# A two-layer decoder trunk on one core: seven products instead of eight for one more column group of the MLP's second eighth, with its fast steps at other places

## The chip, the cores and the metric

The kernel runs on one core of a Trainium2 chip. The metric is the device time of one execution in microseconds (us); of several runs the median is taken. The kernel before takes 2023.53 us, the median of three runs between 2023.32 and 2023.73.

## The reference, cut to what matters

256 tokens of width 2048 pass through two layers. Each has a mixing half (attention heads and gated groups) and an MLP half, and the change touches the MLP alone, D_FF being 8192:

```python
for l in range(DEPTH):
    ...
    h2 = rms_norm(x, norm2_g[l])
    x = x + jnp.square(jax.nn.relu(h2 @ w_up[l])) @ w_down[l]
return rms_norm(x, final_g)
```

Everything is float32, and a product of two float32 matrices is made on TensorE as three products of fp32r parts (high by high, low by high, high by low), so each weight and each activation is split into a high part (`hi`, an ACT copy) and a low part (`lo`, a DVE subtraction).

## The kernel before, in words

**Steps.** The whole program is one list of steps. An ordinary step multiplies one weight tile of 128 x 1024 numbers (512 KB): `Sub.load` issues its DMA on SP (L159), `Sub.high` writes `hi` on ScalarE (ACT, L168), `Sub.low` writes `lo` on VectorE (DVE, L178), and `mm` in `transposed` issues 24 matmuls on TensorE (PE, L410). Column groups of 256 fill one PSUM bank; when the last step of such a group is done, a function (`after`) empties the bank. Weights are prepared a few tiles ahead: there are seven buffers for raw tiles and six each for `hi` and `lo`, and each engine runs its instructions in the order in which the steps' loop wrote them.

**Eighths.** An MLP is worked in eight slices of 1024 hidden units. In round `e` of the loop at the end of `layer`, 16 ordinary steps make the hidden units of eighth `e` from `w_up` (four column groups of four steps, called up steps here), and eighth `e-1` is multiplied with its 1024 rows of `w_down`. For each 256 columns of hidden units, ACT applies relu (L787) and square (L790), and `to_half` makes high (ACT, L646) and low (DVE, L649).

**Fast steps.** A group of 512 output columns of `w_down` can be done by `fast` with seven half-size products instead of eight (a Winograd form of Strassen's scheme over a 2 x 2 split). It is two fast steps of 42 matmuls each (PE, L440) instead of four ordinary steps of 24. Each fast step takes four tiles: two that are loaded (`Top` and `Bottom`), and two made from them by four DVE subtractions (L219, L220, L223, L224), called upper and lower here after the names in `fast`. On the other side it needs sums of the hidden units, made by `sums` (DVE, L803 to L806) and split into high and low in `sum_parts`. The seven products lie in three and a half PSUM banks: the first column group has them in the auxiliary banks, where six add up over the rounds and only the seventh is copied out (L876); each other one uses whichever of the banks acc0 and acc1 the ordinary steps aren't filling at that moment, then acc2 and acc3 (`slots_other`), and half an auxiliary bank for the seventh product.

**What happens to the products.** For the second and third column groups, ACT copies the three banks to the SBUF tile `stage` right behind the second fast step (L908) and the seventh half bank five tiles later (L894). GpSimd (POOL) then adds them to DRAM tiles, `far` (`put`, L873), and in a group's final round adds them back and `combine` forms the outputs. `stage` is one buffer for all groups.

**Places.** `ORDER` and `USUAL` say which column groups are done by fast steps in round `e` and at which places: a pair (7, 9) puts the group's two fast steps ahead of ordinary steps 7 and 9 of that round, counted from 0. Round 1 has two groups before, at places 7 and 10 and at 13 and 14; rounds 2 to 5 follow `USUAL`, with three groups at (7, 9), (2, 3) and (13, 14). Places 0 to 15 are up steps, four to a bank, and the banks alternate between acc0 and acc1; so step 12 begins a new bank, and the bank of steps 8 to 11 is then the one that isn't being filled.

Of the kernel before, what the change touches and what calls it, by code (L numbers as in the profile page):

```python
# [29 lines left out]
F32R = mybir.dt.float32r  # L30
I32 = mybir.dt.int32
AF = mybir.ActivationFunctionType
OP = mybir.AluOpType
AX = mybir.AxisListType

P = 128
# [3 lines left out]
KC = D // P  # L40
NH = 8
# [18 lines left out]

ORDER = {1: ((7, 10), (13, 14)), 6: ((12, 15), (2, 3), (7, 8)), 7: ((7, 10), (2, 3)), 8: ()}
FINAL = (7, 7, 6)
LAST = (4, 6, 8, 10, 0, 2, 12, 14)
USUAL = ((7, 9), (2, 3), (13, 14))
# [25 lines left out]
def trunk(ctx: ExitStack, tc: tile.TileContext, layout, xT, consts, gains, w, b_sp, w_sp, out):  # L92
    nc = tc.nc
# [18 lines left out]
    shared = [None]  # L112
    ar = tp.tile([P, sum(a[1] * a[2] for a in ARENA.values()) - FIRST], F32, name="ar")
    inner_flat = ar[:, 0:2048]
    inner = inner_flat.rearrange("p (k t) -> p k t", k=NH)
# [3 lines left out]
    def new_shared(dtype):  # L119

        shared[0] = tp.tile([P, FIRST], dtype, name="shared", tag="shared", bufs=1)
# [106 lines left out]
    cols = cp.tile([P, (2 * DEPTH + 1) * KC + 2 * DEPTH * NH], F32, name="cols")  # L228
# [14 lines left out]
    def later(delay, cost, fn):  # L243

        queue.append((now[0] + delay, cost, fn))
# [118 lines left out]
    summed, sum_parts = [True], [None]  # L364
# [4 lines left out]
    def collect(fn, *args, **kw):  # L369
        n = len(steps)  # L370
        fn(*args, **kw)
        part = steps[n:]
        del steps[n:]
        return part
# [100 lines left out]
    def mark(fn):  # L475

        steps.append((None, fn, None))
# [4 lines left out]
    def from_tiles(tiles, n):  # L482
        return lambda k: tiles[k // n][0][:, k % n, :, :]

    def new_half(cell):
        cell[0] = tp.tile([P, NH, 2, S], F32R, name="half", tag="half", bufs=2)
# [15 lines left out]
    def pair(ps):  # L502
        return ps.rearrange("p (a b) -> p a b", a=2)
# [14 lines left out]
    def layer(l, n1, n2, n3, last):  # L518
# [125 lines left out]
        def to_half(t, c, src, wait=False):  # L644

            act.activation(t[:, c:c + 2, 0, :], src, AF.Copy)  # L646

            def low():
                vec.tensor_tensor(t[:, c:c + 2, 1, :], src, t[:, c:c + 2, 0, :].bitcast(F32), op=OP.subtract)  # L649

            if wait:
                behind.append((now[0] + 1, low))
            else:
                low()
# [98 lines left out]
        def wide(t):  # L753
            return t[:, None, :].to_broadcast([P, 2, S])
# [8 lines left out]
        def after_down(e, c, ps):  # L763

            if e == 8:
                update(n3, c, ps, True, last)
            elif c < 12:
                vec.tensor_tensor(pair(ps), pair(ps), wide(n2.R2), op=OP.mult)
                update(n3, c, ps, False, last)
            elif e == 1:  # L770
                act.activation(rest_sums[:, c - 12:c - 10, :], pair(ps), AF.Copy)
            else:
                y = rest_sums[:, c - 12:c - 10, :]
                vec.tensor_tensor(y, y, pair(ps), op=OP.add)
# [6 lines left out]
        def after_up(e):  # L781
            def f(c, ps):
                if hid[e][0] is None:
                    new_half(hid[e])
                z = inner[:, c // P:c // P + 2, :]
                if e < 7:
                    act.activation(z, pair(ps), AF.Relu)  # L787
                else:
                    vec.scalar_tensor_tensor(z, pair(ps), 0.0, wide(n2.R), op0=OP.max, op1=OP.mult)
                act.activation(z, z, AF.Square)  # L790
                to_half(hid[e][0], c // P, z, True)
                if c == 768:
                    summed[0] = False
                    if e == 0:
                        new_shared(F32R)
                        sum_parts[0] = shared[0].rearrange("p (k h t) -> p k h t", k=NH, h=2)
                    later(1, 1.5, sums)
            return f

        def sums():  # L800

            a11, a12, a21, a22 = (inner[:, 4 * k:4 * k + 4, t * P:(t + 1) * P] for t in range(2) for k in range(2))
            vec.tensor_tensor(a22, a21, a22, op=OP.add)  # L803
            vec.tensor_tensor(a21, a11, a21, op=OP.subtract)
            vec.tensor_tensor(a11, a22, a11, op=OP.subtract)
            vec.tensor_tensor(a12, a12, a11, op=OP.subtract)  # L806

            def parts(k):
                to_half(sum_parts[0], k, inner[:, k:k + 2, :])
                summed[0] = k == 6  # L810

            for k in range(0, 8, 2):
                later(0, 0.6, lambda k=k: parts(k))

        def combine(place, c, banks, o=None):

# [46 lines left out]
        def slots_other(g, banks):  # L863
            seventh = sevenths()[g - 1]
            banks[:] = [acc_bank(1 - bank_at[0]), acc_bank(2), acc_bank(3)]
            return [h for b in banks for h in halves(b)] + [seventh]

        far = [dp.tile([P, 256 if g == 0 else 7 * 256], F32, name=f"far{l}{g}") for g in range(3)]

        def put(e, g, r):  # L870

            src = stage[:, r] if g else stage_one
            nc.gpsimd.dma_start(far[g][:, r], src, **({} if e == max(g, 1) else {"accum_op": OP.add}))  # L873

        def seventh_out(e, o):
            act.activation(stage_one, o[6], AF.Copy)  # L876
            put(e, 0, slice(0, 256))

        def first_done(e):
            def f(o):  # L880
                if e < 7:
                    soon(5, lambda: seventh_out(e, o))
                else:
                    soon(10, lambda: nc.gpsimd.dma_start(stage[:, 1536:1792], far[0]))
                    soon(15, lambda: combine(stage, 0, [aux_bank] * 2, o))
                    for i, c in enumerate((12, 14)):
                        soon(17 + 2 * i, lambda c=c: rest_in(c))
            return f

        def other_done(e, g, banks):  # L890
            here = [lambda i=i: acc_bank(i) for i in (2, 3)]

            def rest(o):
                act.activation(stage[:, 1536:1792], o[6], AF.Copy)  # L894
                for i in range(4):
                    soon(2 * i, lambda r=slice(512 * i, min(512 * (i + 1), 1792)): move(r))
                if e == FINAL[g]:
                    soon(9, lambda: combine(stage, 4 * g, here))

            def move(r):  # L900
                if e < FINAL[g]:
                    put(e, g, r)
                else:
                    nc.gpsimd.dma_start(stage[:, r], far[g][:, r], accum_op=OP.add)

            def f(o):
                for i in range(3):
                    act.activation(stage[:, 512 * i:512 * (i + 1)], banks[i], AF.Copy)  # L908
                soon(5, lambda: rest(o))
            return f  # L910

        base = len(steps)
        for e in range(9):
            up, down, quick = [], [], []
            if e == 8:
                mark(lambda: bank_at.__setitem__(0, 1))
            if e < 8:
                up = collect(transposed, "w_up", l, 0, KC, e * 1024, 1024, from_hs, after_up(e), of=2)
            if e:
                w = 512 * len(ORDER.get(e, USUAL))  # L920
                hidden = [hid[e - 1]]
                down = collect(transposed, "w_down", l, (e - 1) * 1024, 8, w, D - w, from_tiles(hidden, NH),
                               lambda c, ps, e=e, w=w: after_down(e, (c + w) // P, ps),
                               apart=last and e == 8, of=2 if e < 8 else 4,
                               cols=None if e < 8 else [c * P for c in LAST])
                for g, at in enumerate(ORDER.get(e, USUAL)):
                    banks = []
                    quick += zip(at, collect(fast, "w_down", l, (e - 1) * 1024, 512 * g, hidden,
                                             (lambda g=g, banks=banks: slots_other(g, banks)) if g else slots_first,
                                             (0, 2, 4, 6) if g or e == 1 else (6,), range(7) if g or e == 7 else (6,),  # L930
                                             other_done(e, g, banks) if g else first_done(e)))
            quick = dict(quick)
            for i, one in enumerate(up + down):
                if i in quick:
                    steps.append(quick[i])
                steps.append(one)
# [13 lines left out]
    for l in range(DEPTH):  # L950
        layer(l, norms[2 * l], norms[2 * l + 1], norms[2 * l + 2], l == DEPTH - 1)
# [80 lines left out]
    n = norms[-1]  # L1032
# [3 lines left out]
    for c, w in [(0, 1), (1, 1)] + [(c, 2) for c in range(2, KC, 2)]:  # L1036
        r = slice(c, c + w)
# [38 lines left out]
```

## Time and profile before

| | |
|---|---|
| median of the runs | 2023.53 us (2023.32 to 2023.73) |
| the profiled execution's own time | 2023.7 us |
| its span, first to last instruction | 2021.9 us |
| mean granted TensorE clock | 0.997 |
| busy: PE, DVE, ACT, POOL | 99%, 78%, 60%, 8% of the span |

The profile is one execution. Between the span and that execution's own time lie 1.8 us. Times in the rows are microseconds from the span's start; a row of a timeline or of the chain gives start, length, engine, line, operation, and a bracket for idle time ahead of it and what ended it. Matmuls overlap each other, so PE shows as busy while it is fed without a gap; how fast it runs is read from many matmuls in a row. The numbering of the lines is that of the kernel before; from L792 on the changed kernel's numbers are 2 to 4 higher.

### The profile page before, as it was taken

What the parts mean: (1) busy time and instruction counts of PE and PEld (TensorE: products, weight loads), DVE (VectorE), ACT (ScalarE), POOL (GpSimd) and SP (SyncE); (2) the same over time, 40 slices, a digit from 0 to 9 for tenths busy, and PEclk for the clock granted to TensorE, in tenths of its full rate; (3) what the DMA queues carried; (4) which work ended last, traced back from release to release, by engine and by line L of the source; (5) the groups of instructions that cost most, each with busy time, mean ns of one, the idle gap of its engine ahead of it and who ended that gap; (6) DMA issues with size and microseconds to landing.
All of it is one profiled execution on the core that took longest, in us unless ns stands there. A gap on an engine that the chain in (4) does not pass through costs nothing.

```text
span 2021.9 us, 40716 instructions
## 1 busy us (share of the span) xinstructions
PE 2009.5 (99%) x16810; PEld 1973.4 (98%) x16810; DVE 1579.8 (78%) x1954; ACT 1221.2 (60%) x1613; POOL 156.2 (8%) x200
## 2 busy tenths in 40 slices
PE   9999999999999999999999999999999999999997
PEld 8998999999999999999989989999999999999997
DVE  7566766688888898898856667667888898888985
ACT  7565455566566666665645654556666666667653
POOL 0002300000001000100000032000000000010000
PEclk9999999999999999999999999999999999999998
DMA  9555556566678776866664555565676776777662
GB/s 330 192 167 167 187 189 202 174 229 204 222 219 239 240 225 203 249 215 215 201 215 158 168 187 188 188 199 179 217 229 208 228 236 216 239 220 241 212 215 81
DMA packets 126442, 419.26 MB, mean 207 GB/s; under 512 B 14128, under 2 KB 22064, under 8 KB 126256
## 3 DMA queue, kind: packets, MB, share of 16 engines
q1 hardware_dynamic: 110800, 389.86, 57.2%
q0 software_dynamic: 14304, 23.86, 6.5%
q8 instruction: 131, 2.15, 0.4%
q10 hardware_dynamic: 1152, 2.94, 0.4%
q14 instruction: 55, 0.45, 0.1%
HBM read 394.58 MB, written 22.02 MB: 206 GB/s over the span
## 4 chain that ended last, share of the span: by engine, by line
PE 99%; DVE 0%; ACT 0%; issue 0%; DVEq 0%
PE acc L410 70%; PE acc L440 10%; PE aux L440 8%; PE acc L470 3%; PE acc L472 3%; PE acc L471 3%; PE aux L699 0%; PE aux L635 0%; PE aux L593 0%; PE aux L622 0%; PE aux L994 0%; DVE x L1038 0%; PE aux L596 0%; PE aux L637 0%; PE acc L846 0%; PE aux L539 0%
## 5 line engine op out<-in xcount | busy, mean ns | idle before, releaser
L168 ACT ACTIVATE hi<-raw 128x1024 fp32r<-128x1024 f32 (+1 forms) x817 | 836.9, 1050 | 487.5 <-DVE raw L220 216.2
L178 DVE TENSOR_TENSOR lo<-raw,hi 128x1024 fp32r<-128x1024 f32 (+1 forms) x817 | 965.3, 1214 | 143.4 <-ACT hi L168 140.4
L410 PE MATMUL acc<-hs,hi 128*128 128x256 f32 x5632 | 985.9, 277 | 0.0
L410 PEld LDWEIGHTS acc<-hs,hi 128*128 128x128 f32 x5632 | 857.9, 188 | 0.4 <-issue 0.2
L410 PE MATMUL acc<-hs,lo 128*128 128x256 f32 x2816 | 778.0, 276 | 0.0
L410 PEld LDWEIGHTS acc<-hs,lo 128*128 128x128 f32 x2816 | 528.7, 188 | 0.4 <-issue 0.2
L410 PE MATMUL acc<-half,hi 128*128 128x256 f32 x2688 | 462.2, 276 | 0.0
L410 PEld LDWEIGHTS acc<-half,hi 128*128 128x128 f32 x2688 | 406.7, 188 | 0.0
L410 PE MATMUL acc<-half,lo 128*128 128x256 f32 x1344 | 371.0, 276 | 0.0
L410 PEld LDWEIGHTS acc<-half,lo 128*128 128x128 f32 x1344 | 252.3, 188 | 0.0
L873 POOL DMA_DIRECT2D far<-ar x92 | 74.2, 816 | 1164.4 <-ACT ar L876 563.9
L440 PE MATMUL acc<-hi,shared 128*128 128x256 f32 x768 | 138.4, 276 | 0.0
L440 PEld LDWEIGHTS acc<-hi,shared 128*128 128x128 f32 x768 | 119.2, 188 | 0.0
L440 PE MATMUL aux<-hi,half 128*128 128x256 f32 x528 | 110.6, 276 | 0.0
L440 PE MATMUL acc<-lo,shared 128*128 128x256 f32 x384 | 106.0, 276 | 0.0
L649 DVE TENSOR_TENSOR half<-ar,half 128x512 fp32r<-128x512 f32 x72 | 49.8, 691 | 68.6 <-ACT half L646 68.6
L470 PE MATMUL acc<-hi,hs 128*128 128x512 f32 x256 | 101.8, 398 | 0.0
L472 PE MATMUL acc<-hi,hs 128*128 128x512 f32 x256 | 100.6, 393 | 0.0
L471 PE MATMUL acc<-lo,hs 128*128 128x512 f32 x256 | 100.3, 392 | 0.0
L440 PEld LDWEIGHTS aux<-hi,half 128*128 128x128 f32 x528 | 87.2, 188 | 0.0
L440 PE MATMUL aux<-hi,shared 128*128 128x256 f32 x448 | 80.7, 276 | 0.0
L510 DVE TENSOR_TENSOR x<-x,acc 128x512 f32<-128x512 f32 (+1 forms) x49 | 33.1, 675 | 59.1 <-PE acc L410 57.3
(150 smaller groups left out, 1955.3 us busy)
## 6 DMA issues: line engine op xcount, KB each, us to landing
raw<-in_w SPq DMA_DIRECT2D x731, 512.0 KB, 4.7
far<-ar POOLq DMA_DIRECT2D x60, 256.0 KB, 8.3
far<-ar POOLq DMA_DIRECT2D x32, 128.0 KB, 4.3
ar<-far POOLq DMA_DIRECT2D x12, 256.0 KB, 9.7
raw<-in_w SPq DMA_DIRECT2D x10, 256.0 KB, 5.1
x<-in_xT SPq DMA_DIRECT2D x7, 256.0 KB, 5.9
out<-x SPq DMA_DIRECT2D x7, 256.0 KB, 3.1
shared<-in_b_sp ACTq DMA_DIRECT2D x2, 512.0 KB, 7.7
```

Of the source, the lines that this page charges most:

```text
L168: act.activation(self.h[:, j * m:(j + 1) * m], self.raw[:, j * m:(j + 1) * m], AF.Copy)
L178: vec.tensor_tensor(lo[:, r], self.raw[:, r], self.h[:, r].bitcast(F32), op=OP.subtract)
L410: pe.matmul(o, lhsT=lhs, rhs=xs[:, rhs, :], start=(first and j == 0), stop=(last and j == 2), skip_group_check=True)
L440: calls.append(lambda k=k, j=j, lhs=lhs, rhs=rhs: pe.matmul(o[n], lhsT=lhs, rhs=rhs, start=(p == 0 and k == 0 and j == 0 and n in fresh), ...
L470: pe.matmul(ps, lhsT=xh, rhs=hi, start=(k0 + k == 0), stop=False)
L471: pe.matmul(ps, lhsT=xh, rhs=lo, start=False, stop=False)
L472: pe.matmul(ps, lhsT=xl, rhs=hi, start=False, stop=(k0 + k == KC - 1))
L510: vec.tensor_tensor(xj, xj, ps[j][:, 0:S] if alone else pair(ps)[:, j, :], op=OP.add)
L649: vec.tensor_tensor(t[:, c:c + 2, 1, :], src, t[:, c:c + 2, 0, :].bitcast(F32), op=OP.subtract)
L873: nc.gpsimd.dma_start(far[g][:, r], src, **({} if e == max(g, 1) else {"accum_op": OP.add}))
```

## The change

The third column group (output columns 1024 to 1535) is done by seven products in round 1 too, in both layers. The three groups of that round stand at places 2 and 5, 9 and 10, 13 and 14. Since the first fast step comes 2 instead of 7 steps behind the last relu of round 0, round 0 makes its hidden columns in the order 0, 512, 256, 768, and its sums of activations are made in two parts: those for the first fast step after column 512, the others after 768. In `put`, round 1 now writes the third group's products to `far` and round 2 adds to them, where round 2 wrote them before.

```diff
-ORDER = {1: ((7, 10), (13, 14)), 6: ((12, 15), (2, 3), (7, 8)), 7: ((7, 10), (2, 3)), 8: ()}
+ORDER = {1: ((2, 5), (9, 10), (13, 14)), 6: ((12, 15), (2, 3), (7, 8)), 7: ((7, 10), (2, 3)), 8: ()}
...
+                if e == 0 and c == 512:
+                    new_shared(F32R)
+                    sum_parts[0] = shared[0].rearrange("p (k h t) -> p k h t", k=NH, h=2)
+                    later(1, 1.0, lambda: sums([0]))
                 if c == 768:
                     summed[0] = False
-                    if e == 0:
-                        new_shared(F32R)
-                        sum_parts[0] = shared[0].rearrange("p (k h t) -> p k h t", k=NH, h=2)
-                    later(1, 1.5, sums)
+                    later(1, 1.5, lambda: sums([0, 1] if e else [1]))
             return f
...
-        def sums():
-
-            a11, a12, a21, a22 = (inner[:, 4 * k:4 * k + 4, t * P:(t + 1) * P] for t in range(2) for k in range(2))
+        def sums(ps):
+
+            n, i = 2 * len(ps), 2 * ps[0]
+            a11, a12, a21, a22 = (inner[:, 4 * k + i:4 * k + i + n, t * P:(t + 1) * P] for t in range(2) for k in range(2))
...
             for k in range(0, 8, 2):
-                later(0, 0.6, lambda k=k: parts(k))
+                if k % 4 // 2 in ps:
+                    later(0, 0.6, lambda k=k: parts(k))
...
-            nc.gpsimd.dma_start(far[g][:, r], src, **({} if e == max(g, 1) else {"accum_op": OP.add}))
+            nc.gpsimd.dma_start(far[g][:, r], src, **({} if e == 1 else {"accum_op": OP.add}))
...
-                up = collect(transposed, "w_up", l, 0, KC, e * 1024, 1024, from_hs, after_up(e), of=2)
+                up = collect(transposed, "w_up", l, 0, KC, e * 1024, 1024, from_hs, after_up(e), of=2,
+                             cols=None if e else (0, 512, 256, 768))
```

Counted over the whole program, PE has 24 matmuls fewer, DVE 24 operations more, ACT 16 more and POOL 8 DMAs more.

Two places show how this moves instructions. The first is ACT from the second fast step at place 10 of round 1 to the relu of hidden columns 512 to 767, first layer. Before, the fast step at place 10 is of the first group and leaves nothing for ACT to copy at once; `hi_4627` and `hi_4673` are ordinary steps 11 and 12, and `hi_4675`, `hi_4677`, `hi_4689` and `hi_4723` are top, bottom, upper and lower of place 13. The last row empties the bank of steps 8 to 11 (acc1):

```order
L168 ACTIVATE hi_4627<-raw_4436 128x1024
L168 ACTIVATE hi_4673<-raw_4466 128x1024
L186 ACTIVATE hi_4675<-raw_4532 128x512
L168 ACTIVATE hi_4677<-raw_4534 128x1024
L168 ACTIVATE hi_4689<-raw_4532 128x1024
L168 ACTIVATE hi_4723<-raw_4534 128x1024
L876 ACTIVATE ar_80<-aux_4471 128x256
L787 ACTIVATE ar_80<-acc1_4572 128x512
```

In the changed kernel the fast step at place 10 is the second group's, and its three banks are copied first (L911, L908 before). `hi_4817` is step 12, `hi_4819`, `hi_4821`, `hi_4833` and `hi_4867` are the four tiles of place 13, and L897 copies the seventh product of place 10:

```order
L911 ACTIVATE ar_80<-acc0_4675 128x512
L911 ACTIVATE ar_80<-acc2_4676 128x512
L911 ACTIVATE ar_80<-acc3_4677 128x512
L168 ACTIVATE hi_4817<-raw_4608 128x1024
L186 ACTIVATE hi_4819<-raw_4642 128x512
L168 ACTIVATE hi_4821<-raw_4673 128x1024
L168 ACTIVATE hi_4833<-raw_4642 128x1024
L168 ACTIVATE hi_4867<-raw_4673 128x1024
L897 ACTIVATE ar_80<-aux_4319 128x256
L787 ACTIVATE ar_80<-acc1_4644 128x512
L790 ACTIVATE ar_80<-ar_80 128x512
```

The three copies now stand ahead of step 12's `hi`, of all four of place 13's and of the relu that empties acc1. The products of place 13 go to acc1 in both kernels (acc1_4796 before, acc1_4941 now), so its first matmul needs that relu done.

The second place is DVE behind the last relu of round 0, first layer. Before, all sums are made there (L803 to L806 on 128x4x128), with `lo_4270` and `lo_4304` of the two ordinary steps that follow, and only then the first tile of the first fast step (`lo_4338`, its top):

```order
L649 TENSOR_TENSOR half_3852<-ar_80,half_3852 128x2x256
L803 TENSOR_TENSOR ar_80<-ar_80 128x4x128
L804 TENSOR_TENSOR ar_80<-ar_80 128x4x128
L805 TENSOR_TENSOR ar_80<-ar_80 128x4x128
L806 TENSOR_TENSOR ar_80<-ar_80 128x4x128
L178 TENSOR_TENSOR lo_4270<-raw_4047,hi_4232 128x1024
L649 TENSOR_TENSOR shared_4231<-ar_80,shared_4231 128x2x256 x2
L178 TENSOR_TENSOR lo_4304<-raw_4077,hi_4268 128x1024
L649 TENSOR_TENSOR shared_4231<-ar_80,shared_4231 128x2x256 x2
L191 TENSOR_TENSOR lo_4338<-raw_4111,hi_4302 128x512
```

In the changed kernel the second half of the sums (L805 to L808 on 128x2x128) stands between the upper tile (`lo_4242`) and the lower tile (`lo_4278`) of the fast step at place 2:

```order
L223 TENSOR_TENSOR raw_3987<-raw_3987,raw_3952 128x2x256
L224 TENSOR_TENSOR raw_3987<-raw_3987 128x2x256
L178 TENSOR_TENSOR lo_4242<-raw_3952,hi_4209 128x1024
L649 TENSOR_TENSOR half_3852<-ar_80,half_3852 128x2x256
L805 TENSOR_TENSOR ar_80<-ar_80 128x2x128
L806 TENSOR_TENSOR ar_80<-ar_80 128x2x128
L807 TENSOR_TENSOR ar_80<-ar_80 128x2x128
L808 TENSOR_TENSOR ar_80<-ar_80 128x2x128
L178 TENSOR_TENSOR lo_4278<-raw_3987,hi_4240 128x1024
L649 TENSOR_TENSOR shared_3981<-ar_80,shared_3981 128x2x256 x2
```

So the fast step's tiles have moved ahead of the sums, and its last one stands behind them.

## The prediction

> **What bounds the kernel now.** I read the page's busy times and its chain of waits first. The columns are busy time, share of the span and instructions; below them is the chain's share by engine.
>
> ```profile
> PE   2009.5 (99%) x16810; PEld 1973.4 (98%) x16810; DVE 1579.8 (78%) x1954; ACT 1221.2 (60%) x1613; POOL 156.2 (8%) x200
> PE 99%; DVE 0%; ACT 0%; issue 0%; DVEq 0%
> ```
>
> PE is fed for 99% of the span and is 99% of the chain that ends last. Busy does not mean that it never waits, so the table of waits of PE comes next (total, times, longest):
>
> ```profile
> PE aux L328 <- DVE nr L354: 1.2, 1, 1.2
> PE aux L994 <- DVE warm L990: 1.1, 1, 1.1
> ```
>
> These are the program's first and last waits; in between, PE waits for nobody. So a matmul that goes is gained in full, and a wait that comes is lost in full. The third view is the table of windows over rounds 1, 2 and 3 of the first layer (window, length, busy time of PE, PEld, DVE, ACT and POOL with counts, granted clock, DMA share, GB/s); I set the borders by the chain.
>
> ```profile
> 376.76:461.17 84.41, 84.41 (x747) 84.41 (x746) 72.06 (x84) 54.50 (x69) 2.96 (x5) 1.00 0.59 201
> 461.17:544.25 83.08, 83.08 (x734) 83.08 (x734) 69.46 (x78) 54.41 (x69) 6.60 (x9) 1.00 0.72 227
> 544.25:627.33 83.08, 83.08 (x734) 83.08 (x734) 72.79 (x83) 54.80 (x69) 7.83 (x9) 1.00 0.73 227
> ```
>
> Rounds 2 and 3 have the three fast groups that round 1 is to get, and run 1.33 us shorter, with DVE at 72.8 of 83.08 us and no wait of PE. That bears out the amount of work, not the new places.
>
> **Part 1, the products.** Four ordinary steps (96 matmuls) become two fast steps (84). The chain merges matmuls of a line (start, length, what); the first row is 96 ordinary matmuls, the others are the fast steps at places 10 and 13 of round 1:
>
> ```profile
> 93.84 10.90 PE acc L410 x96
> ...
> 408.75 4.54 PE aux L440 x40
> ...
> 421.69 4.08 PE acc L440 x36
> ```
>
> Both kinds cost the same each: 10.90 / 96 = 113.5 ns and 4.08 / 36 = 113.3 ns. Twelve fewer are 1.36 us a layer, 2.72 us in all. The outputs' last part (combine and its transposes) is there already for this group, so PE gains no new work. From here an ordinary step is 24 matmuls, 2.72 us, and a fast one 42, 4.76 us.
>
> **Part 2, sums at place 2.** The last relu of round 0 and what follows it on ACT, then a DVE operation of 256 columns, the size of the halved sums:
>
> ```profile
> 376.80 0.60 ACT L787 ACTIVATE ar<-acc 128x512 f32<-128x512 f32 x1 [1.66 <-PE acc L410]
> 377.43 0.63 ACT L790 ACTIVATE ar<-ar 128x512 f32<-128x512 f32 x1
> 378.09 0.63 ACT L646 ACTIVATE half<-ar 128x512 fp32r<-128x512 f32 x1
> ```
>
> ```profile
> 2006.41 0.42 DVE L510 TENSOR_TENSOR x<-x,acc 128x256 f32<-128x256 f32 x1 [2.00 <-PE acc L410]
> ```
>
> ACT has the high part done at 378.7. On DVE follow its low part (0.69, the size of an L219 row below), four half sums (4 x 0.42) and the lower tile of place 2 (1.22, an L178 row below): about 382.4. PE begins place 2 two steps after 376.76, at 382.2, and needs the lower tile for the sixth product, 30 matmuls (3.4 us) later, at 385.6. That leaves 3.2 us; the second sums aren't read before place 5. Eight halves for four whole sums cost DVE 0.6 us of its spare time. I take 0; below zero nothing can come, for PE doesn't wait there now; were the second parts needed by the third product, it would be 0.1 us.
>
> **Part 3, a new wait at place 13.** The first product of place 13 writes the bank of steps 8 to 11, so its first matmul waits until relu L787 has read that bank. On ACT that relu stands behind all four tiles of place 13 in both kernels. Before, this was in time:
>
> ```profile
> 415.95 1.06 ACT L168 ACTIVATE hi<-raw 128x1024 fp32r<-128x1024 f32 x1 [2.70 <-DVE raw L220]
> 417.40 1.06 ACT L168 ACTIVATE hi<-raw 128x1024 fp32r<-128x1024 f32 x1 [0.39 <-DVE raw L224]
> 418.37 0.36 ACT L876 ACTIVATE ar<-aux 128x256 f32<-128x256 f32 x1
> 419.00 0.60 ACT L787 ACTIVATE ar<-acc 128x512 f32<-128x512 f32 x1 [0.27 <-PE acc L410]
> ```
>
> ```profile
> 421.52 0.28 PE L440 MATMUL acc<-hi,half 128*128 128x256 f32 x1
> ```
>
> The relu ended at 419.6, 1.9 us ahead of that matmul, and only PE kept it waiting. Now the three copies L911 stand between place 10 and place 13 on ACT, three steps ahead instead of four or more. How ACT and DVE go on after such copies is seen in round 6, place 3 (chain, then ACT, then DVE):
>
> ```profile
> 806.43 4.08 PE acc L440 x36
> ```
>
> ```profile
> 810.54 0.60 ACT L908 ACTIVATE ar<-acc 128x512 f32<-128x512 f32 x1 [0.76 <-PE acc L440]
> 811.04 2.00 ACT L168 ACTIVATE hi<-raw 128x1024 fp32r<-128x1024 f32 x2
> 812.94 0.62 ACT L186 ACTIVATE hi<-raw 128x512 fp32r<-128x512 f32 x1
> 813.45 1.05 ACT L168 ACTIVATE hi<-raw 128x1024 fp32r<-128x1024 f32 x1
> ```
>
> ```profile
> 812.12 2.36 DVE L178 TENSOR_TENSOR lo<-raw,hi 128x1024 fp32r<-128x1024 f32 x2 [2.04 <-ACT hi L168]
> 814.40 0.69 DVE L191 TENSOR_TENSOR lo<-raw,hi 128x512 fp32r<-128x512 f32 x1
> 815.00 1.22 DVE L178 TENSOR_TENSOR lo<-raw,hi 128x1024 fp32r<-128x1024 f32 x1
> 816.14 0.69 DVE L219 TENSOR_TENSOR raw<-raw 128x512 f32<-128x512 f32 x1
> 816.86 0.69 DVE L220 TENSOR_TENSOR raw<-raw 128x512 f32<-128x512 f32 x1
> ```
>
> I count from the start of place 10 on PE. The third copy waits for the sixth product and starts at 810.54 - 806.43 = 4.11. Step 12's `hi` starts 0.50 later, at 4.61, and ends at 5.66; its `lo` starts at 5.69 (812.12 against 811.04 + 1.05), the top's `lo` 1.14 later at 6.83 (two took 2.28), the bottom's 0.60 later at 7.43, L219 at 8.57, L220 at 9.29 to 9.98. The upper `hi` starts at 10.02, the lower 1.45 later (417.40 - 415.95) at 11.47, the copy of the seventh product 0.97 later at 12.44, and the relu 0.36 later at 12.80, to end at 13.40. PE is ready at 421.52 - 408.75 = 12.77. So it waits 0.63, and with the handing over about 0.7 us, once a layer: 1.4 us. Bounds: 0, if the relu gets through as before; and 0.9, if the upper tile comes 0.2 us later than in round 6. I take 0.7, since each link has its row.
>
> The Trainium skill (Perfetto Trace Analysis, section Optimizing Tensor Performance, Matmuls) wants independent groups to rotate through PSUM banks so that emptying one overlaps the next group's matmuls; kept here it would give no wait and a sum of -2.72 us. The rows above speak for the wait: the overlap is there, but the bank is asked for again three steps after the copies.
>
> At place 14 both move together. Its first matmul comes 429.19 - 421.69 = 7.50 us after place 13's, its upper tile 18 matmuls later:
>
> ```profile
> 427.57 4.77 DVE L178 TENSOR_TENSOR lo<-raw,hi 128x1024 fp32r<-128x1024 f32 x4
> ```
>
> ```profile
> 429.19 4.08 PE acc L440 x36
> ```
>
> The upper `lo` ended at 427.57 + 1.19 = 428.76, 9.76 after the relu's start; counted as above 22.56, against PE's 13.45 + 7.50 + 2.04 = 22.99. It still gets through, by 0.4 us.
>
> **Part 4, DMAs and `stage`.** The added puts wait on POOL with nothing but puts behind them. Issue to landing of the present 92:
>
> ```profile
> DMA to landing us min/median/max: 2.9/7.6/11.3
> ```
>
> ACT may write `stage` again at place 14 once the second group's puts have read it. The last of the three big ones is issued by about 6 us after place 10 starts and lands by 17.2 at the latest seen; the copies of place 14 start at 12.94 + 7.50 + 1.4 = 21.9. Cost 0. SP's weight loads wait for buffers that DVE frees, not for DMA:
>
> ```profile
> SPq L159 <- DVE lo L178: 1626.4, 706, 10.0
> ```
>
> **The sum.** -2.72 + 1.4 = -1.3 us. The profiled execution of 2023.7 (span 2021.9 and 1.8 around it) becomes 2022.4; it lies 0.2 over the median of 2023.53, which becomes **2022.2 us**. A change of 0.2%, 4.05 us, is about what a measurement of this kernel can tell from none; this one is 0.07%.
>
> **The rivals.**
>
> *No wait at place 13.* The relu gets through and the whole 2.72 us are kept: 2020.8. For it: PE shows no wait in any round now. Against it: no round now has bank copies three steps ahead of a place that asks for a bank.
>
> *VectorE becomes the bound between places 9 and 14: slower than before.* Four fast steps with five ordinary ones between stand there. By the rows, a fast step is 0.69 + 3 x 1.22 + 4 x 0.69 = 7.1 us of DVE, an ordinary one 1.22, a low part 0.69: 35.2 us against 4 x 4.76 + 5 x 2.72 = 32.6 us of PE. Most of the 2.6 us is worked ahead; the row at 812.12 shows DVE 2.04 us idle there. If nothing is ahead, DVE ends some 0.6 us late, and if it carries over a further 0.9 us from places 2 and 5, place 13 waits 0.7 + 0.9 = 1.6 us a layer: 2020.8 + 3.2 = 2024.0. It turns slower than before where the wait passes 1.36 us.
>
> *The wait costs PE its clock.* Windows at the program's end, then the first matmuls:
>
> ```profile
> 2009.40:2010.60 1.20, 0.01 (x1) 0.00 (x0) 0.71 (x5) 0.30 (x2) 0.00 (x0) 1.00 0.00 0
> 2010.60:2011.80 1.20, 1.17 (x4) 0.88 (x4) 0.00 (x0) 0.00 (x0) 0.00 (x0) 0.54 0.00 0
> ```
>
> ```profile
> 6.38 0.63 PE L471 MATMUL acc<-lo,hs 128*128 128x512 f32 x1
> 6.81 0.52 PE L472 MATMUL acc<-hi,hs 128*128 128x512 f32 x1
> 7.17 0.39 PE L470 MATMUL acc<-hi,hs 128*128 128x512 f32 x1
> 7.40 0.40 PE L471 MATMUL acc<-lo,hs 128*128 128x512 f32 x1
> ```
>
> Behind 1.2 us of idle PE the granted clock is 0.54. At the start, matmuls come 0.43 us apart up to about 7 us and 0.23 us apart afterwards, so up to 6 us at some 0.53 of the speed. Were the wait at place 13 to bring such a stretch, it would cost up to 6 x 0.47 = 2.8 us a layer: 2022.2 + 5.6 = 2027.8. Against it: this wait is half as long, with dense matmuls on both sides, where the one at the end lies behind single-column matmuls. The Trainium skill (TensorE: Matmul & The Clock Gate, section HAM oscillation) has the clock fall only for idle gaps beyond about 3.4 us; the 0.54 behind 1.2 us shows that less can do.
>
> **How the numbers follow.** Forecast 0.73; no wait 0.12; DVE the bound 0.08; the clock 0.05; a gain beyond any term here 0.02. The range is to leave out only the last two: 2020.6, a little under no wait, to 2024.0, where DVE is the bound; the forecast's own bounds (0.5 to 0.9 us a wait) give 2021.8 to 2022.6. Faster by over 0.2% has no term: 0.02. Slower by over 0.2% is the clock's case: 0.05. The rest, 0.93, lies within.
>
> **What would show it.** Right: PE's table of waits has two new entries, L440 waiting for ACT `ar` L787, 0.5 to 0.9 us each, at place 13 of round 1 in both layers, and PE has 24 matmuls fewer. No such entry: the first rival. Entries above 1.36 us, or DVE without idle time behind L911: the second. A granted clock below 1.00 behind place 13: the third. An entry at place 2, or waits of ACT for `far` at L911, would prove parts 2 or 4 wrong; a median outside 2020.6 to 2024.0 the whole.

## The result, and the profile after

The changed kernel takes **2055.85 us** (2055.44 to 2056.28, 4 runs), the kernel before 2023.5 beside it: 1.016 times as long, 95% interval 1.0142 to 1.0177. The forecast was 2022.2, so 33.7 us have to be explained. The profiled execution's own time is 2055.44, its span 2053.7 us.

The page of the changed kernel, busy times and the chain's shares by engine:

```profile
PE 2040.1 (99%) x16786; PEld 2002.8 (98%) x16786; DVE 1595.0 (78%) x1978; ACT 1233.8 (60%) x1629; POOL 162.6 (8%) x208
PE 98%; DVE 1%; ACT 0%; DMA 0%; issue 0%; ACTq 0%; DVEq 0%
```

PE has 24 matmuls fewer, as forecast, is still busy for 99% and still bounds the program, yet it is busy for 30.6 us more. So it is not idle time that came in: the matmuls themselves come more slowly. The table of waits of PE (total, times, longest) has the forecast entry, and it is short:

```profile
PE aux L328 <- DVE nr L354: 1.2, 1, 1.2
PE aux L998 <- DVE warm L994: 1.1, 1, 1.1
PE acc L440 <- ACT ar L787: 1.0, 2, 0.5
PE acc L470 <- ACT hs L287: 0.5, 1, 0.5
```

Place 13 of round 1 waits for the relu once a layer. (L470 is one wait in the first layer's first microseconds.) ACT around that place, from the third bank copy on, and then PE (timelines):

```profile
422.43 0.60 ACT L911 ACTIVATE ar<-acc 128x512 f32<-128x512 f32 x1 [0.76 <-PE acc L440]
...
429.88 1.06 ACT L168 ACTIVATE hi<-raw 128x1024 fp32r<-128x1024 f32 x1 [0.39 <-DVE raw L224]
430.84 0.36 ACT L897 ACTIVATE ar<-aux 128x256 f32<-128x256 f32 x1
431.10 0.59 ACT L787 ACTIVATE ar<-acc 128x512 f32<-128x512 f32 x1
```

```profile
430.98 0.28 PE L410 MATMUL acc<-hs,hi 128*128 128x256 f32 x1
431.75 0.39 PE L440 MATMUL acc<-hi,half 128*128 128x256 f32 x1 [0.49 <-ACT ar L787]
431.97 0.28 PE L440 MATMUL acc<-lo,half 128*128 128x256 f32 x1
```

The next matmul would have started at 430.98 + 0.11 = 431.09 and started at 431.75: 0.66 us lost. The table says 0.49 because it counts from a modelled end. What comes behind is seen in the chain, which merges the matmuls of a line (start, length, what). The rows with x36 are the same work before the wait, behind it, and much later:

```profile
410.81 4.08 PE acc L440 x36
...
418.32 4.09 PE acc L440 x36
...
431.75 4.51 PE acc L440 x36
...
439.80 4.24 PE acc L440 x36
...
879.16 5.55 PE acc L410 x47
...
899.22 4.08 PE acc L440 x36
```

36 matmuls take 4.08 us ahead of the wait, 4.24 behind it (117.8 ns each instead of 113.3), and 4.08 again at 899; the row at 431.75 is longer because it holds the restart, with 0.22 us between its first two matmuls. The border lies at 884.7, at the first four transposes of `combine` in round 6 (matmuls of 128 x 128):

```profile
884.71 0.44 PE acc L849 x4
885.15 5.46 PE acc L410 x48
```

47 matmuls ahead of them took 5.55 us, 48 behind them take 5.46. The windows of these stretches (columns as in the prediction), of the changed kernel and then of the kernel before:

```profile
341.40:422.40 81.00, 81.00 (x716) 81.00 (x716) 61.85 (x72) 49.94 (x64) 1.77 (x3) 1.00 0.57 183
431.80:884.50 452.70, 452.70 (x3840) 452.70 (x3841) 384.16 (x434) 295.13 (x372) 40.55 (x49) 1.00 0.72 222
885.10:952.00 66.90, 66.90 (x592) 66.90 (x591) 61.77 (x77) 41.71 (x52) 4.98 (x6) 1.00 0.67 223
```

```profile
431.80:860.00 428.20, 428.20 (x3775) 428.20 (x3775) 372.15 (x423) 281.96 (x355) 38.97 (x48) 1.00 0.73 228
```

Length by PE's count is the number to read here: 113.1, **117.9** and 113.0 ns a matmul in the changed kernel, 113.4 before. The granted clock is 1.00 in all four, and PE is busy throughout in all four. The second layer shows the same from 1448.5 to 1901.5. I call the two the short pace and the long pace. Their difference is 452.70 / 3840 - 428.20 / 3775 = 4.46 ns, times 3840 = **17.1 us a layer**. The sum: -2.7 for the products, 2 x 0.66 for the waits, 2 x 17.1 for the pace: +32.9, against 2055.85 - 2023.5 = +32.4 measured.

That is an account of where the time lies, not yet of its cause: round 1 has one more fast group, other places and a wait, and each could be what changes the pace.

### The profile page after: what moved, and what is told of

It reads as the page before. It is cut to its first block, busy times and chain, and to the rows that moved or that the text cites. A ratio compares the mean times of both kernels' runs of the same rounds, so it can differ in the third digit from the quotient of the medians.

```text
span 2053.7 us, 40733 instructions
## 1 busy us (share of the span) xinstructions
PE 2040.1 (99%) x16786; PEld 2002.8 (98%) x16786; DVE 1595.0 (78%) x1978; ACT 1233.8 (60%) x1629; POOL 162.6 (8%) x208
## 4 chain that ended last, share of the span: by engine, by line
PE 98%; DVE 1%; ACT 0%; DMA 0%; issue 0%; ACTq 0%; DVEq 0%
PE acc L410 68%; PE acc L440 11%; PE aux L440 8%; PE acc L472 3%; PE acc L470 3%; PE acc L471 3%; PE aux L699 0%; PE aux L635 0%; PE aux L593 0%; PE aux L622 0%; DVE x L1042 0%; ACT hi L168 0%; DMA cols<-in_gains 0%; PE aux L596 0%; PE aux L637 0%
## 5 line engine op out<-in xcount | busy, mean ns | idle before, releaser
L410 PE MATMUL acc<-hs,hi 128*128 128x256 f32 x5632 | 1003.8, 279 | 0.0
L410 PE MATMUL acc<-half,hi 128*128 128x256 f32 x2560 | 444.9, 278 | 0.0
L410 PEld LDWEIGHTS acc<-half,hi 128*128 128x128 f32 x2560 | 388.6, 188 | 0.0
L410 PE MATMUL acc<-half,lo 128*128 128x256 f32 x1280 | 355.0, 277 | 0.0
L410 PEld LDWEIGHTS acc<-half,lo 128*128 128x128 f32 x1280 | 241.8, 189 | 0.0
L440 PE MATMUL acc<-hi,shared 128*128 128x256 f32 x832 | 154.5, 279 | 0.0
L440 PEld LDWEIGHTS acc<-hi,shared 128*128 128x128 f32 x832 | 130.4, 188 | 0.0
L440 PE MATMUL aux<-hi,half 128*128 128x256 f32 x544 | 116.5, 279 | 0.0
L440 PE MATMUL acc<-lo,shared 128*128 128x256 f32 x416 | 115.9, 279 | 0.0
L470 PE MATMUL acc<-hi,hs 128*128 128x512 f32 x256 | 101.6, 397 | 0.5 <-ACT hs L287 0.5
L440 PEld LDWEIGHTS aux<-hi,half 128*128 128x128 f32 x544 | 90.4, 188 | 0.0
L440 PE MATMUL acc<-hi,half 128*128 128x256 f32 x416 | 81.8, 280 | 1.0 <-ACT ar L787 1.0
L440 PE MATMUL aux<-hi,shared 128*128 128x256 f32 x448 | 82.8, 278 | 0.0
```

The source lines that it names most:

```text
L410: pe.matmul(o, lhsT=lhs, rhs=xs[:, rhs, :], start=(first and j == 0), stop=(last and j == 2), skip_group_check=True)
L440: calls.append(lambda k=k, j=j, lhs=lhs, rhs=rhs: pe.matmul(o[n], lhsT=lhs, rhs=rhs, start=(p == 0 and k == 0 and j == 0 and n in fresh), ...
L470: pe.matmul(ps, lhsT=xh, rhs=hi, start=(k0 + k == 0), stop=False)
```

## The experiments

The theory: the wait alone does it. A short wait in a stream of 128x256 matmuls leaves PE at the long pace until small matmuls come by, so its price is its own length plus 4.5 ns for each matmul on the way. The rivals: the new load does it (a third fast group, more DVE work and DMAs, other places); and, for the end of the stretch, that it ends by time or by round and the small matmuls only happen to stand there.

**1. The change without its wait** (later_place). The third pair moves by one place, so that the relu is through before the bank is asked for:

```diff
-ORDER = {1: ((2, 5), (9, 10), (13, 14)), ...
+ORDER = {1: ((2, 5), (9, 10), (14, 15)), ...
```

> The changed kernel with the third group one place later, at 14 and 15, so that the relu that empties the bank of steps 8 to 11 has one more ordinary step (2.7 us) and PE should not wait there; all else is as changed. Theory (pace): PE has two paces, 113.4 and 117.9 ns a matmul; starting again after the 0.5 us wait at place 13 leaves it on the slower one until the small matmuls of L849, and that is the 32 us. Then no wait means no slow pace: 24 matmuls fewer and nothing else, 2020.8 us (2020.5 to 2021.1). Rival (layout or traffic: the two-part sums, the other column order, three groups in round 1 or the added DMAs slow the matmuls themselves): the slow pace stays, about 2055.

Measured: **2020.66 us** (2020.03 to 2020.95, 11 runs; before 2023.44), 0.9985 times, interval 0.9976 to 0.9994. PE's first matmul of that pair comes at 433.87, 2.4 us after the relu's end at 431.43, and L440 has no entry in the waits. The window:

```profile
431.80:860.00 428.20, 428.20 (x3775) 428.20 (x3774) 376.60 (x429) 286.20 (x362) 40.42 (x48) 1.00 0.73 227
```

3775 matmuls in 428.2 us, as in the kernel before, with the same three groups, the same products and DMAs as the changed kernel. So the extra load isn't the cause. This version is faster than both kernels.

**2. The wait without the change** (before_wait). The kernel before, with three ACT copies ahead of the relu that empties the bank in round 1; their result isn't used:

```diff
+                if e == 1 and c == 512:
+                    for _ in range(3):
+                        act.activation(stage[:, 0:1024], con, AF.Copy)
```

> The kernel before with nothing of the change; in round 1 three ACT copies of 128x1024 (1 us each, into a part of the staging tile that isn't in use yet) are put ahead of the relu that empties the bank of steps 8 to 11, so that PE waits some 0.3 to 1 us at place 13, once a layer. Theory (pace): the wait alone makes the slow stretch up to round 6: 2023.5 + 1.4 + 2 x 17 = 2059 us (2055 to 2061). Rival (layout or traffic): only the waits are added, 2024 to 2025.5.

Measured: **2059.62 us** (2059.32 to 2060.15, 4 runs), 1.0178 times, interval 1.0164 to 1.0192. Its waits and its windows behind the wait and behind round 6's transposes:

```profile
PE acc L440 <- ACT ar L790: 1.4, 2, 0.7
```

```profile
422.90:886.50 463.60, 463.60 (x3936) 463.60 (x3937) 390.97 (x441) 299.60 (x376) 39.12 (x48) 1.00 0.71 219
887.00:950.00 63.00, 63.00 (x557) 63.00 (x556) 58.61 (x73) 39.67 (x51) 4.97 (x6) 1.00 0.67 215
```

117.8 ns a matmul up to the transposes, 113.1 behind them, in a kernel whose work and order on PE are those of before. 1.4 us of waits cost 36.2 us. With experiment 1 this settles what sets the long pace off at place 13: the wait is enough, and without it the change doesn't do it.

**3. The change with two fast groups in round 1** (two_groups), as a check on the new places without the third group and without a wait:

```diff
+ORDER = {1: ((2, 5), (13, 14)), ...
...
+            nc.gpsimd.dma_start(far[g][:, r], src, **({} if e == max(g, 1) else {"accum_op": OP.add}))
```

> The changed kernel with its two-part sums, its column order in round 0 and the first group at places 2 and 5, but without the third group in round 1: the second group stays at 13 and 14, and the third group's DMAs are as before. The copies of a second group then don't stand ahead of place 13. Theory (pace): no wait, no slow pace, and the work of before: 2023.5 us (2023.2 to 2023.8). Rival (the two-part sums or the column order slow the matmuls): about 2055.

Measured: 2023.25 us (2023.08 to 2024.55, 10 runs), 1.0 times, interval 0.999 to 1.0009. PE has no wait there, and the MLP of both layers runs at the short pace. Places 2 and 5, the split sums and the other order of columns cost nothing that shows.

**4. and 5. The length of the wait** (waits_a, waits_b). As experiment 2, with copies of other sizes in the two layers:

```diff
+                    for m in ((1024, 1024, 512), (1024, 1024, 1024, 256))[l]:
+                        act.activation(stage[:, 0:m], con[:, 0:m], AF.Copy)
```

waits_b has (1024, 1024, 768) and (1024, 1024, 1024, 1024) there.

> The kernel before with ACT copies ahead of the relu of place 13, as before_wait, but of other lengths: in the first layer 2.5 copies (a wait of PE of some 0.3 us), in the second 3.25 (some 1.1 us); before_wait had 0.7 us in both. Theory (every wait): any wait inside the dense stream leaves PE at 117.9 ns a matmul up to round 6, 17.4 us a layer: 2023.4 + 1.4 + 34.8 = 2059.6 us, slow in both layers. Rival (phase): the pace after a wait depends on where in some cycle PE starts again, so one length or the other leaves 113.4 ns: 2042 us with one slow layer, 2025 with none.

> As waits_a, with 2.75 copies in the first layer (a wait of some 0.5 us) and 4 in the second (some 1.7 us). Theory (every wait): 2023.4 + 2.2 + 34.8 = 2060.4 us, slow in both layers. Rival (phase): 2043 us with one slow layer, 2025.6 with none.

Measured, one run each: 2060.8 us with waits of 0.3 and 1.2 us, 2062.01 with 0.5 and 1.8. With experiment 2 that makes 2059.6, 2060.8 and 2062.0 us for 1.4, 1.5 and 2.3 us of waits in all, and all six layers run at the long pace up to round 6. A wait of 0.3 us is followed by the same long pace, worth 17 us, as one of 1.8: in this range the length of the wait isn't what sets the pace.

The longest wait brought something more. These are windows behind the wait of 1.8 us, in the second layer of waits_b, where PE starts again at 1441.84:

```profile
1441.90:1443.10 1.20, 1.20 (x10) 1.20 (x11) 0.00 (x0) 1.17 (x3) 0.00 (x0) 1.00 0.01 3
1443.10:1446.60 3.50, 3.50 (x19) 3.50 (x18) 3.20 (x4) 2.42 (x4) 0.00 (x0) 0.51 0.13 18
1446.70:1450.00 3.30, 3.30 (x30) 3.30 (x30) 3.20 (x6) 1.13 (x2) 0.00 (x0) 1.00 0.35 139
```

For 3.4 us the granted clock was half, and in PE's timeline 15 matmuls from 1443.29 to 1446.49 start 213 ns apart, 1.4 us more than at the long pace. Then the clock is 1.00 again and the pace still the long one. So the clock's fall, the third rival of the prediction, came behind this wait, and it is a thing apart from the long pace. Behind the other waits in the MLPs of these kernels, of up to 1.3 us, the clock stayed at 1.00.

**6. Small matmuls soon behind the wait** (small_four). The changed kernel, with four transposes of a 128 x 128 identity into a free bank behind place 14 of round 1; their result isn't used:

```diff
+                if e == 1 and g == 2:
+                    soon(2, small)
+
+            def small():
+                ps = acc_bank(2)
+                for n in range(4):
+                    pe.transpose(ps[:, n * P:(n + 1) * P], ident, ident)
```

> The changed kernel, wait and all, with four 128x128 matmuls of the identity (transposes, the shape of L849) added in each layer, two ordinary steps or so behind place 14 of round 1; their result isn't used. Theory (pace): they set PE back to 113.4 ns, so only some 180 matmuls a layer run slow: 2023.5 - 2.7 + 1.0 for the two waits + 1.6 for the slow stretches + 0.9 for the added matmuls = 2024.3 us (2023.5 to 2025). Rival (layout or traffic): added matmuls change nothing, 2056 to 2057.

Measured: **2028.35 us** (2027.8 to 2029.13, 9 runs), 1.0024 times, interval 1.0014 to 1.0033. The waits are those of the changed kernel. The chain around the four transposes, here L908:

```profile
447.04 8.38 PE acc L410 x71
455.41 0.44 PE acc L908 x4
```

and the window from there to round 6:

```profile
459.00:880.00 421.00, 421.00 (x3712) 421.00 (x3711) 370.65 (x424) 279.29 (x356) 39.13 (x45) 1.00 0.73 226
```

118.0 ns ahead of them, 113.4 behind them. So the stretch ends neither by time nor by round: 0.44 us of small matmuls gave back some 16 us a layer. But the time is 4 us over the expectation, and the chain shows why, in the attention of both layers. There the kernel before has a piece of its own at the long pace. It begins behind eight matmuls of the attention (four of L593, 0.22 us each, and four of 128x128, L596) and ends at six transposes (L622; the 96 matmuls behind them stand in the prediction, at 93.84, with 10.90 us):

```profile
58.79 21.79 PE acc L410 x192
80.57 0.86 PE aux L593 x4
81.44 0.44 PE aux L596 x4
81.88 11.31 PE acc L410 x96
93.19 0.65 PE aux L622 x6
```

That is 113.5 ns a matmul ahead of the eight and 117.8 behind them, with no wait of PE there in the table. So a wait is enough for the long pace, but it isn't the only thing that brings it; every kernel run here has this piece, in both layers. In small_four the same six didn't end it:

```profile
82.10 11.31 PE acc L410 x96
93.41 0.66 PE aux L622 x6
94.07 11.31 PE acc L410 x96
```

The piece went on to 151.5, 528 matmuls instead of 96: 432 x 4.5 ns = 1.9 us a layer. With that the sum closes: -2.8 (experiment 1) + 1.3 of waits + 2 x 0.8 for the 21.5 us up to the transposes + 0.9 for the transposes + 3.9 = 4.9, measured 4.9. It also shows that small matmuls don't always bring the short pace back. Which way it goes isn't drawn anew in each execution: the nine runs of small_four lie within 1.4 us of each other.

**7. to 9. Which small matmuls** (small_few, small_odd, small_alone). The code of experiment 6 with one small matmul in layer 1 and two in layer 2; with three and five; and, on the kernel of experiment 1, which has no wait, four 128 x 128 in layer 1 and four of a single column in layer 2:

```diff
+                for n in range(1 + l):
...
+                for n in range(3 + 2 * l):
...
+                    if l == 0:
+                        pe.transpose(ps[:, n * P:(n + 1) * P], ident, ident)
+                    else:
+                        pe.matmul(ps[:, n:n + 1], lhsT=ident, rhs=ones[:, 0:1], start=(n == 0), stop=True,
+                                  skip_group_check=True)
```

> The changed kernel with its waits, and behind place 14 of round 1 one 128x128 matmul in the first layer and two in the second, instead of four in both as in small_four. Theory (any small matmul sets PE back): 2024 us, or 2028 if the slow stretch in the attention that small_four showed (17.4 us would be a whole round's part; there it was some 430 matmuls more a layer, 1.9 us) comes too. Rival (it takes four, or it is a matter of phase): one layer or both stay slow up to round 6, 16.6 us each: 2041 or 2057.

> As small_few, with three 128x128 matmuls in the first layer and five in the second: one left PE slow, two and four brought it back to 113.4 ns. Theory (two or more do): slow only for some 170 matmuls behind place 13 in both layers, 2024 to 2025 us, and up to 4 us more if one of the slow stretches of small_four or small_few comes elsewhere. Rival (an odd number leaves it slow): slow up to round 6 in both layers, 2056 to 2057.

> The kernel later_place, which has no wait, with small matmuls added behind the third group of round 1: four of 128x128 in the first layer, four with a single column (the shape of L320) in the second. Theory (the shape decides): behind the 128x128 ones PE goes on at 113.4 ns, behind the single-column ones at 117.9 ns up to round 6, since the stretch behind L320 is slow in every trace so far: 2020.7 + 0.6 + 16.5 = 2037.8 us, slow in the second layer alone. Rival (only waits slow PE): 2021.3 us, neither layer slow.

Measured, one run each, so that one, two, three and five small matmuls were each tried in one layer: 2042.33, 2026.39 and 2025.47 us. The chain of small_few in layer 1, then in layer 2:

```profile
453.13 0.11 PE acc L908
453.24 2.83 PE acc L410 x24
```

```profile
1470.02 0.22 PE acc L908 x2
1470.24 9.78 PE acc L410 x86
```

One left the long pace as it was (117.9 ns behind it, up to 884.7), two ended it (113.7). So it isn't true that any small matmul ends it. Three and five ended it too, so an odd number isn't the reason. Small matmuls without a wait ahead, of either shape, left the short pace as it was, so the shape alone doesn't set it. The attention's piece was long in one of the two layers of small_odd and of small_alone and short in the other (of small_alone's 4.8 us over experiment 1 that piece makes 1.9, the added matmuls 0.9 and a wait of L470 in the first microseconds 1.4; 0.6 stay unexplained), and in layer 2 of small_few the four transposes of round 6, which ended the long pace wherever it reached them, met the short pace and were followed by the long one from 1886.1 to 1948.8, again with no wait. What decides is something that these counts and shapes don't name.

**10. and 11. A second wait, and a wait in a late round** (second_wait, wait_rounds). As experiment 2, by rounds, with copies of a constant tile onto itself:

```diff
+                if e in (1, 3) and c == 512:
+                    for _ in range(3):
...
+                if c == 512:
+                    for _ in range(({1: 3, 3: 5}, {5: 4})[l].get(e, 0)):
```

> The kernel before with three ACT copies of 1 us (a constant tile onto itself) ahead of the relu of place 13 in round 1, as before_wait, and again in round 3. Theory (a wait always leaves PE slow): the second wait, some 0.3 to 0.7 us beside a matmul stream that is slow already, changes nothing: slow from round 1 to round 6 in both layers, 2023.4 + 2.6 + 34.8 = 2060.8 us (2059 to 2062). Rival (a wait draws the pace anew): at 113.4 ns from round 3 on in one layer or both, 2048 or 2035 us.

> The kernel before with ACT copies ahead of the relu of place 13: in the first layer three in round 1 and five in round 3 (in second_wait three there came too early to make PE wait), in the second layer four in round 5 alone. Theory (a wait leaves PE at 117.9 ns until small matmuls come): a first layer slow from round 1 to round 6 through both waits, 0.7 + 1.5 + 17.5 us; a second layer slow only from round 5 to the small matmuls of round 6, some 910 matmuls, 1.0 for the wait + 4.1: 2048.3 us (2047 to 2050). Rival (each wait draws the pace anew): the first layer at 113.4 ns from round 3 on, 2037 us, or the second not slow, 2044. Rival (the cost of a wait is the same wherever it stands): 17 us in the second layer too, 2061.

In second_wait (2059.82 us, one run) three copies were too few in round 3: the relu was through in time, and the run only repeats experiment 2. In wait_rounds (2048.16 us, one run) layer 1 waits in rounds 1 and 3, layer 2 in round 5 alone. The waits, and two windows of layer 2, ahead of that wait and from it to the transposes:

```profile
PE acc L440 <- ACT ar L790: 2.5, 3, 1.3
```

```profile
1362.20:1780.00 417.80, 417.80 (x3684) 417.80 (x3684) 350.94 (x393) 271.49 (x342) 28.25 (x36) 1.00 0.69 220
1786.50:1893.50 107.00, 107.00 (x910) 107.00 (x909) 92.72 (x107) 72.59 (x94) 10.40 (x12) 1.00 0.74 221
```

113.4 and 117.6 ns. The wait of round 5 costs its length and 107 us at the long pace, 4 us instead of 17. In layer 1 the second wait, 1.3 us long and met at the long pace, left it so, up to 888.6. So the price of such a wait is set by how far away the next small matmuls are that end the long pace.

Over all these kernels 18 waits of 0.3 to 1.8 us in the dense stream met the short pace, and each of the 18 left the long one behind it. All of them are at one place, the first matmul of place 13, and end with the same relu on ACT; a wait at another instruction, or for another engine, wasn't tried.

## Why the prediction was wrong, point by point

**Part 1, the products: right.** Forecast -2.72 us for 24 matmuls; experiment 1, which has them and no wait, gives 2020.66 - 2023.44 = -2.8.

**Part 2, the sums: right.** DVE at place 2 of the changed kernel:

```profile
380.88 0.42 DVE L808 TENSOR_TENSOR ar<-ar 128x256 f32<-128x256 f32 x1
381.22 1.22 DVE L178 TENSOR_TENSOR lo<-raw,hi 128x1024 fp32r<-128x1024 f32 x1
```

The lower tile is ready at 382.4, as worked out, and nothing of place 2 stands in the table of waits.

**Part 3, the wait: right in place, number, cause and length.** The relu ended 431.69 - 418.32 = 13.37 us after place 10's start, forecast 13.40; PE lost 0.66 us, forecast 0.7. Place 14 waits for nothing, as forecast.

**Part 4, DMAs and `stage`: right.** PE waits for nothing but the four entries above, and the copies of L911 waited for nothing but PE's L440 (64 times, 0.8 us at most), not for a DMA.

**The step that failed** is the sentence behind the first table of waits: "So a matmul that goes is gained in full, and a wait that comes is lost in full." The first half holds. The wait here costs its length and then 4.46 ns for each of the matmuls up to the next small ones, 3840 here: 0.66 + 17.1 us, not 0.7. Every term of the sum was about right, and the one that carried the result wasn't in it.

**The rivals.** The third, that the wait costs PE its clock, had the right place for the loss and the wrong thing: it asked for a granted clock below 1.00 behind place 13, and the windows of the changed kernel show 1.00; it priced 6 us at half speed, 2.8 us a layer, where some 450 us ran at 96% of the speed and cost 17.1. The Trainium skill (TensorE: Matmul & The Clock Gate, section HAM oscillation) gives the rule as no idle gaps of PE beyond about 3.4 us. The traces agree with it for waits of 0.3 to 1.3 us, behind which the clock stays at 1.00, and not for the one of 1.8 us in waits_b, behind which it fell to half. Nor can the rule be read as saying that shorter gaps are free: the waits of 0.5 us here were followed by 17 us of loss each. No wait (the first rival) is what experiment 1 brought about, at its price. DVE as the bound (the second) fell: the waits are 0.5 us and not above 1.36, and DVE had 2.55 us of idle time behind L911, ahead of its row at 424.01.

**What could have been read beforehand.** The chain of the kernel before has the row at 81.88, quoted in experiment 6: 96 matmuls in 11.31 us, right ahead of the row at 93.84 that the prediction quotes, 96 in 10.90. The same work at two paces, 117.8 and 113.5 ns, at a granted clock of 1.00 on this core, with other matmuls at both borders and no wait. That would have given a rival a price: if the wait brings the long pace and it lasts to the transposes of round 6, some 3840 x 4.3 ns = 16.5 us a layer, 2022.2 + 33 = 2055. The prediction took its price from the short-pace row and passed over its neighbour.

**What stays open.** Why PE has two paces, and what state a wait leaves behind: clock, busy share and DMA share are the same. One thing in the records goes with the pace. Of the weight loads between 446 and 860 us, grouped by line and tiles, those of one matmul in three of the up steps last 188 ns in the kernel before and 192 in the changed kernel (the columns behind the shapes are count, busy time, mean in ns and idle time):

```profile
L410 PEld LDWEIGHTS acc<-hs,lo 128*128 128x128 f32 x632 | 118.6, 188 | 0.0
L410 PEld LDWEIGHTS acc<-hs,lo 128*128 128x128 f32 x619 | 118.7, 192 | 0.0
```

Without the wait (later_place, 460 to 860 us) it is 188 again. In the attention's piece of the kernel before, from 82 to 93 us, other loads are the longer ones (`hs,hi`, 190 on average, 188 in the piece behind it). This marks the pace; that it causes it isn't shown. It is open, too, which small matmuls end the long pace: two to five did behind these waits and one didn't, the six transposes of the attention did in some kernels and not in others, and small matmuls can also bring the long pace in. A wait much shorter than 0.3 us, and matmuls of another size, weren't tried.

## What to carry to other kernels

In a kernel whose TensorE is never idle, price a new wait not only by its length but also by what the stream behind it may lose, up to the next change in its pattern, and look for the pace (length by number of matmuls in merged rows of the chain, or in windows), since the busy share and the granted clock show nothing of it. Look for it in the kernel that you have, too. An edit that gains little by fewer matmuls should first be placed so that no matmul waits: moved by one place, this change runs at 0.9985 of the time before (0.9976 to 0.9994) instead of 1.016. Where a wait can't be avoided, try it late, close ahead of small matmuls that the program has anyway: in round 5 it cost 4 us instead of 17.

## What the hardware showed that I had not expected

A stream of fp32r matmuls of 128x256, each with its own weight load, has two steady paces at a granted clock of 1.00, 113.4 and 117.9 ns. A wait of 0.3 us is enough to go from the first to the second, 450 us don't end it, and two transposes of 0.11 us each did, while one didn't. Eight matmuls of the attention, without a wait, brought it in as well (from 80.57 in the kernel before). And a wait of 1.8 us, not one of 1.3, was followed by 3.4 us at half the granted clock.
